# ln2's gain and bias for six of eight row tiles: from VectorE to GpSimd

## The chip, the cores and the metric

One NeuronCore of one Trainium2 chip. The metric is the device time of one execution in microseconds (us), the median over runs. Engines are named as the profile names them: PE is TensorE's matmul, PEld its weight load, DVE is VectorE, ACT is ScalarE, POOL is GpSimd, SP is the sync engine, which here only issues DMAs.

## The reference, cut to what matters

One post-norm layer over 1024 positions of width 1024, all in float32. The change lies in the very last step, the second residual update and its layer norm:

```python
y = (jax.nn.silu(a) * val) @ w_down[l]
x = _layer_norm(alpha * x + (1.0 + g2) * y, ln2_g[l], ln2_b[l])
```

`_layer_norm` takes mean and variance of each row over the 1024 columns, then `(x - mu) * rsqrt(var + eps) * gain + bias`. The gain `ln2_g` and the bias `ln2_b` are vectors over the columns; the kernel holds each of them copied to all 128 partitions, as `l2g` and `l2b` (128x1024 float32 each, in SBUF).

## The kernel before, in words

Everything up to the activation of the channel mixing (normalisation, projections, two attentions, merge, output projection, first residual norm, up-projection, convolution, gate) stands before the change and isn't touched. GpSimd's last work there is four DMA issues at 1334 to 1337 us; from then on its queue is empty to the end.

The down-projection that follows, from about 1337 us on, is one level of a fast matrix product: seven products P1, P5, P6, P3, P2, P7, P4 in place of eight, each over 11 pairs of operands (an activation block and a weight block or a sum of such, 128x512 each). A product's result is four tiles of 128 rows by 512 columns in PSUM (`psd`), in one of two sets of four banks; P1, P6, P7 and P4 add up in the same four banks.

Each operand is loaded from DRAM by SP (`rw`, nine buffers, line 1270) and split in two float32r parts in `op` (20 buffers, that is ten pairs): ScalarE writes the high part (line 1265, CAST), VectorE the low part (line 1266, `rw` minus the high part). Each pair then costs twelve matmuls: for each of the four row tiles high x high (line 1276), high x low (1277) and low x high (1278).

In the order in which the work is written, a product ends with line 1390, where VectorE adds the PSUM result to a kept tile. The rows of the output are 8 tiles `yt` of 128 rows by 1024 columns. P3 and P2 complete the two halves of row tiles 0 to 3, P7 the right half of tiles 4 to 7, P4 their left half. What follows from P3, P2 and P7 is put in a list (`later`), of which one entry is written after each pair of the next product: `part` (line 1314 gain `g2row`, line 1315 residual, line 1339 row statistics) and, for tiles 0 to 3, `finish`. P4's last nine pairs are handled tile by tile: all nine pairs for row tile 4, then for 5, 6, 7 (27 matmuls each), and behind each tile its left half (lines 1375, 1376, 1377) and its `finish`.

`finish` for tiles 0 to 5 is: some operations on 128x1 statistics (lines 121 to 139), ScalarE's normalisation of the whole 128x1024 tile in place (line 140), and then on VectorE a multiplication by `l2g` (line 1320) and an addition of `l2b` (line 1321), each 128x1024, in place. SP stores the tile (line 1331). For tiles 6 and 7 VectorE does the whole in two fused steps on halves (lines 1326 and 1327) and SP and ScalarE store a half each (line 1328).

A scheduler reads the written program and sets, ahead of the run, the order of the instructions on each engine; on the chip each engine then works through its own list in order. So what stands in front of an instruction in its engine's list delays it. Two dependences matter below. PE may start P4 on a PSUM bank only when line 1390 of P7 has read that bank, since P4 adds to the same bank. And line 1277 of a pair needs the low part that line 1266 wrote.

Of the kernel before, what the change touches and what calls it, by code (L numbers as in the profile page):

```python
# [15 lines left out]
ALU = mybir.AluOpType  # L16
# [28 lines left out]
def body(ctx, tc, a, out):  # L45
    nc = tc.nc
    ve, se, pe, po, sy = nc.vector, nc.scalar, nc.tensor, nc.gpsimd, nc.sync
# [67 lines left out]
    def norm_scale(src, n=2, st=None):  # L115
        if st is None:
            st = small.tile([P, n, 6], F32, name=nm("st"), tag=f"st{n}", bufs=4 if n == 2 else 1)
            for i in range(n):
                ve.bn_stats(out=st[:, i, :], in_=src[:, i * D // n : (i + 1) * D // n])
        mv = small.tile([P, 2], F32, name=nm("mv"), tag="mv")  # L120
        ve.bn_aggr(out=mv, in_=st.rearrange("p a b -> p (a b)"))
        v = small.tile([P, 1], F32, name=nm("v"), tag="v")
        ve.tensor_scalar_add(v, mv[:, 1:2], EPS)
        sd = small.tile([P, 1], F32, name=nm("sd"), tag="sd")
        se.activation(out=sd, in_=mv[:, 1:2], func=AF.Sqrt, bias=epst[:, 0:1])
        y = small.tile([P, 1], F32, name=nm("y"), tag="y")
        ve.reciprocal(out=y, in_=sd)
        t = small.tile([P, 1], F32, name=nm("t"), tag="t")
        ve.scalar_tensor_tensor(out=t, in0=y, scalar=v, in1=y, op0=ALU.mult, op1=ALU.mult)
        ve.tensor_scalar(out=t, in0=t, scalar1=-0.5, scalar2=1.5, op0=ALU.mult, op1=ALU.add)  # L130
        r = small.tile([P, 1], F32, name=nm("r"), tag="r")
        ve.tensor_tensor(out=r, in0=y, in1=t, op=ALU.mult)
        return mv, r

    def normalise(dst, src, on_act=False, st=None):
        mv, r = norm_scale(src, 2, st)
        if on_act:
            b = small.tile([P, 1], F32, name=nm("nb"), tag="nb")
            ve.scalar_tensor_tensor(out=b, in0=mv[:, 0:1], scalar=-1.0, in1=r, op0=ALU.mult, op1=ALU.mult)
            se.activation(out=dst, in_=src, func=AF.Identity, scale=r, bias=b)  # L140
        else:
            ve.tensor_scalar(out=dst, in0=src, scalar1=mv[:, 0:1], scalar2=r, op0=ALU.subtract, op1=ALU.mult)
# [53 lines left out]
    def halves(half):  # L196
        return slice(half * H, (half + 1) * H)
# [17 lines left out]
    class Stream:  # L215
# [49 lines left out]
        def finish(self, upto):  # L265
            while self.cur < upto:
                self.step()
# [1028 lines left out]
    with tc.tile_pool(name="dn", bufs=2, reuse_waits="tile") as dn:  # L1296
# [20 lines left out]
        def finish(t, y, st=None):  # L1317
            if t < NT - 2:
                normalise(y, y, True, st)
                ve.tensor_tensor(out=y, in0=y, in1=l2g, op=ALU.mult)  # L1320
                ve.tensor_tensor(out=y, in0=y, in1=l2b, op=ALU.add)
            else:
                mv, r = norm_scale(y, 2, st)
                for n in range(2):
                    ns = halves(n)
                    ve.scalar_tensor_tensor(out=y[:, ns], in0=y[:, ns], scalar=mv[:, 0:1], in1=l2g[:, ns], op0=ALU.subtract, op1=ALU.mult)
                    ve.scalar_tensor_tensor(out=y[:, ns], in0=y[:, ns], scalar=r, in1=l2b[:, ns], op0=ALU.mult, op1=ALU.add)
                    (sy, se)[n].dma_start(out=out[t * P : (t + 1) * P, ns], in_=y[:, ns])
# [12 lines left out]
        for p in products:  # L1341
# [17 lines left out]
            if p == "P5":  # L1359
                l2g = dn.tile([P, D], F32, name="l2g", tag="l2g", bufs=1)  # L1360
                l2b = dn.tile([P, D], F32, name="l2b", tag="l2b", bufs=1)
# [7 lines left out]
            for t in range(4):  # L1369
                for w in ws:  # L1370
                    down(ps, t, w, False, w is ws[-1], not fresh)
                if p == "P4":
                    z = dn.tile([P, H], F32, name=nm("z"), tag="z", bufs=2)
                    y, n0 = ys[4 + t], halves(0)
                    ve.tensor_tensor(out=z, in0=ps[t], in1=g2row[:, n0], op=ALU.mult)
                    ve.scalar_tensor_tensor(out=y[:, n0], in0=y[:, n0], scalar=ALPHA, in1=z, op0=ALU.mult, op1=ALU.add)
                    ve.bn_stats(out=stats[4 + t][:, 0, :], in_=y[:, n0])
                    finish(4 + t, y, stats[4 + t])
                    if t < 2:
                        sent(4 + t, y)  # L1380
            if p == "P1":
                p1 = kept("p1", ps)
            elif p == "P5":
                p5 = kept("p5", ps)
            elif p == "P6":
                u2 = kept("u2", ps)
            elif p in ("P3", "P2", "P7"):
                for t in range(4):
                    x = {"P3": u2, "P2": p1, "P7": p5}[p][t]
                    ve.tensor_tensor(out=x, in0=ps[t], in1=x, op=ALU.add)  # L1390
                    tt, n = {"P3": (t, 1), "P2": (t, 0), "P7": (4 + t, 1)}[p]
                    later.append(lambda tt=tt, n=n, x=x: part(tt, n, x))
                    if p == "P2":
                        later.append(lambda t=t: finish(t, ys[t], stats[t]))
# [65 lines left out]
```

## Time and profile before

| what | us |
|---|---|
| time, median of 3 runs | 1549.76 (1547.07 to 1550.41) |
| span of the profiled execution, first to last instruction | 1548.2 |
| median less the profiled span | 1.6 |
| PE busy, share of the span | 1502.7, 97% |
| DVE busy | 1034.5, 67% |
| ACT busy | 709.5, 46% |
| POOL busy | 658.2, 43% |
| lines 1320 and 1321 on DVE, six each | 7.2 and 7.1 |

The profiled execution is a single one, and its own time is given as the span alone; the time of a run contains what lies around the span too. Busy times are sums over the whole program, in which the stages have quite different limits: POOL's share all lies before 1337 us, and the change lies behind 1486 us. Rows of the timeline give the start, how long the instruction took, the engine, the line, what it writes and reads, and how many of them the row merges ("x4"). A merged row's length runs to the end of its last instruction; neighbours on DVE overlap by some 0.08 us, so the cost of an instruction in a busy stretch is read from start to start.

### The profile page before, as it was taken

The numbers are of one execution on the slowest core, as the hardware profiler recorded it, in microseconds if no ns is written. First come the engines' busy times: TensorE is split into PE (matmuls) and PEld (weight loads), VectorE is DVE, ScalarE is ACT, GpSimd is POOL, SyncE is SP. The second block draws the span as 40 slices with busy tenths as digits, with TensorE's granted clock in tenths as the row PEclk, the third lists the DMA queues.
The fourth block names the chain that finished last, engine by engine and source line by source line (L and its number), as shares of the span: only waits on it lengthen the run. The fifth ranks groups of instructions, "written<-read, shape, count | busy, mean of one in ns | idle before, by whom it ended". The sixth has DMA issues, their size and how long they took to land.

```text
span 1548.2 us, 21760 instructions
## 1 busy us (share of the span) xinstructions
PE 1502.7 (97%) x7663; PEld 1264.7 (82%) x7663; DVE 1034.5 (67%) x2038; ACT 709.5 (46%) x1316; POOL 658.2 (43%) x607
## 2 busy tenths in 40 slices
PE   6999999999999999999998999999999999999996
PEld 3788898889889888888886877888888888888885
DVE  6756566566656565554468587777778776845798
ACT  3545555554544454442112165544544554555451
POOL 0039897787878776730000005454455443000000
PEclk9999999999999999999999999999999999999998
DMA  9156666756576578758999575443344322697552
GB/s 366 50 165 215 217 192 198 218 194 216 189 233 220 189 260 299 260 151 292 308 323 347 214 258 190 140 154 132 122 140 147 115 102 104 246 328 255 191 190 75
DMA packets 129756, 317.54 MB, mean 205 GB/s; under 512 B 13024, under 2 KB 21936, under 8 KB 129648
## 3 DMA queue, kind: packets, MB, share of 16 engines
q1 hardware_dynamic: 90208, 197.83, 37.8%
q0 software_dynamic: 25344, 92.02, 17.8%
q10 hardware_dynamic: 14096, 26.31, 4.8%
q8 instruction: 60, 0.98, 0.3%
q14 instruction: 48, 0.39, 0.1%
HBM read 223.47 MB, written 84.25 MB: 199 GB/s over the span
## 4 chain that ended last, share of the span: by engine, by line
PE 72%; POOL 9%; DMA 8%; DVE 7%; issue 2%; ACT 1%; SPq 0%; ACTq 0%; DVEq 0%; POOLq 0%
PE psu L859 25%; PE psd L1277 4%; PE psd L1278 4%; PE psd L1276 4%; PE pso L508 3%; DMA wod<-dr 3%; PE psg L192 3%; PE psg L194 3%; PE psg L193 3%; POOL dr L553 2%; PE pst L494 2%; POOL acc L559 2%; POOL dr L556 2%; PE psq L194 2%; DMA brd<-dr 2%
## 5 line engine op out<-in xcount | busy, mean ns | idle before, releaser
L859 PE MATMUL psu<-hc,wx 128*128 128x512 f32 x792 | 185.7, 389 | 0.1
L859 PEld LDWEIGHTS psu<-hc,wx 128*128 128x128 f32 x792 | 148.6, 188 | 31.3 <-ACT u L1202 0.5
L1125 DVE SCALAR_TENSOR_TENSOR pcv<-u,convp,pcv 128x1024 f32<-128x1024 f32 x88 | 113.1, 1286 | 45.4 <-ACT pcv L1123 44.4
L1266 DVE TENSOR_TENSOR op<-rw,op 128x512 fp32r<-128x512 f32 x146 | 93.4, 687 | 52.8 <-ACT op L1265 52.5
L1265 ACT CAST op<-rw 128x512 fp32r<-128x512 f32 x146 | 85.2, 622 | 85.4 <-PE psd L1278 39.8
L457 ACT ACTIVATE s<-s,mx 128x640 f32<-128x640 f32 (+7 forms) x128 | 94.5, 738 | 58.6 <-DVE mx L451 57.4
L1277 PE MATMUL psd<-op,op 128*128 128x512 f32 x292 | 113.6, 389 | 0.9 <-DVE op L1266 0.9
L1278 PE MATMUL psd<-op,op 128*128 128x512 f32 x292 | 113.6, 389 | 0.0
L1276 PE MATMUL psd<-op,op 128*128 128x512 f32 x292 | 113.1, 389 | 0.0
L497 ACT CAST pt<-pst 128x512 fp32r<-128x512 f32 (+1 forms) x192 | 82.1, 450 | 62.3 <-PE pst L494 60.8
L498 DVE TENSOR_TENSOR pt<-pst,pt 128x512 fp32r<-128x512 f32 (+1 forms) x192 | 96.0, 519 | 17.2 <-ACT pt L497 15.5
L192 PE MATMUL psq<-h1h,wh 128*128 128x512 f32 x256 | 103.8, 407 | 1.7 <-DVE h1h L188 1.3
L192 PE MATMUL psg<-h1h,wh 128*128 128x512 f32 x256 | 103.7, 405 | 0.0
L194 PE MATMUL psq<-h1h,wl 128*128 128x512 f32 x256 | 100.9, 394 | 0.9 <-DVE wl L112 0.9
L194 PE MATMUL psg<-h1h,wl 128*128 128x512 f32 x256 | 100.3, 392 | 0.5 <-DVE wl L112 0.5
L193 PE MATMUL psq<-h1l,wh 128*128 128x512 f32 x256 | 100.8, 394 | 0.0
L193 PE MATMUL psg<-h1l,wh 128*128 128x512 f32 x256 | 100.2, 391 | 0.0
L556 POOL TENSOR_SCALAR dr<-dr,cond 128x512 f32<-128x512 f32 x56 | 89.9, 1607 | 8.1 <-DMA dr<-in_w_ada 7.1
L508 PE MATMUL pso<-pt,vs 128*128 128x256 f32 x608 | 90.4, 288 | 1.3 <-DVE pt L498 1.2
L994 POOL DMA_DIRECT2D xd<-xr x8 | 4.4, 545 | 199.3 <-DVE xr L992 199.3
L508 PEld LDWEIGHTS pso<-pt,vs 128*128 128x128 f32 x608 | 81.1, 191 | 8.7 <-DVE pt L498 2.6
L112 DVE TENSOR_TENSOR wl<-ws,wh 128x1024 fp32r<-128x1024 f32 x38 | 61.2, 1611 | 39.1 <-ACT wh L111 39.1
(286 smaller groups left out, 4001.3 us busy)
## 6 DMA issues: line engine op xcount, KB each, us to landing
ws<-in_w_up SPq DMA_DIRECT2D x34, 512.0 KB, 3.7
dr<-in_w_ada POOLq DMA_DIRECT2D x32, 512.0 KB, 4.8
dr<-in_w_down POOLq DMA_DIRECT2D x22, 512.0 KB, 4.8
td<-dr POOLq DMA_DIRECT2D x22, 512.0 KB, 4.7
rw<-td SPq DMA_DIRECT2D x44, 256.0 KB, 4.5
yd<-y SPq DMA_DIRECT2D x20, 512.0 KB, 2.7
rw<-yd SPq DMA_DIRECT2D x40, 256.0 KB, 4.2
rw<-sd SPq DMA_DIRECT2D x33, 256.0 KB, 4.6
```

Of the source, the lines that this page charges most:

```text
L192: pe.matmul(ps, wh, xh, start=start, stop=False)
L193: pe.matmul(ps, wh, xl, start=False, stop=False)
L194: pe.matmul(ps, wl, xh, start=False, stop=stop)
L457: se.activation(out=st[:, 0:nk], in_=st[:, 0:nk], func=AF.Exp, scale=-1.0, bias=prev, accum_out=sums[:, col : col + 1])
L498: ve.tensor_sub(out=dl, in0=src, in1=dh)
L508: pe.matmul(ps[:, 0:256], vs[:, h % 2, j0 + j, :], pt[j // 4][:, c, j % 4, :], start=j == 0 and c == 0, stop=j == nj - 1 and c == 1)
L556: po.tensor_scalar_mul(x[:, k % 2, :] if k else acc, x[:, k % 2, :], cond[:, k : k + 1])
L859: pe.matmul(ps, w[:, a_, k, :], h[k][b_], start=first, stop=k == 3 and a_ == 1, skip_group_check=on)
L1125: ve.scalar_tensor_tensor(out=ps, in0=u[b][:, 2 - d : S + 2 - d], scalar=cp[:, 2 - d : 3 - d], in1=ps, op0=ALU.mult, op1=ALU.add)
L1276: pe.matmul(ps[t], g[:, 0, ts], d[:, 0], start=start, stop=False, skip_group_check=on)
L1277: pe.matmul(ps[t], g[:, 0, ts], d[:, 1], start=False, stop=False, skip_group_check=on)
L1278: pe.matmul(ps[t], g[:, 1, ts], d[:, 0], start=False, stop=stop, skip_group_check=on)
```

## The change

Lines 1320 and 1321 are issued to GpSimd (`po`) where they were issued to VectorE (`ve`). Operands, shapes, tiles and results are the same: twelve instructions of 128x1024 float32, each with two inputs in SBUF.

```diff
         def finish(t, y, st=None):
             if t < NT - 2:
                 normalise(y, y, True, st)
-                ve.tensor_tensor(out=y, in0=y, in1=l2g, op=ALU.mult)
-                ve.tensor_tensor(out=y, in0=y, in1=l2b, op=ALU.add)
+                po.tensor_tensor(out=y, in0=y, in1=l2g, op=ALU.mult)
+                po.tensor_tensor(out=y, in0=y, in1=l2b, op=ALU.add)
             else:
```

The scheduler orders the end of the program anew. On POOL, behind the last DMA issue, the list now holds these rows; `yt_13419` to `yt_13425` are row tiles 0 to 3, `yt_13427` and `yt_13429` are tiles 4 and 5:

```order
+L1320 TENSOR_TENSOR yt_13419<-yt_13419,l2g 128x1024
+L1321 TENSOR_TENSOR yt_13419<-yt_13419,l2b 128x1024
+L1320 TENSOR_TENSOR yt_13421<-yt_13421,l2g 128x1024
+L1321 TENSOR_TENSOR yt_13421<-yt_13421,l2b 128x1024
+L1320 TENSOR_TENSOR yt_13423<-yt_13423,l2g 128x1024
+L1321 TENSOR_TENSOR yt_13423<-yt_13423,l2b 128x1024
+L1320 TENSOR_TENSOR yt_13425<-yt_13425,l2g 128x1024
+L1321 TENSOR_TENSOR yt_13425<-yt_13425,l2b 128x1024
+L1320 TENSOR_TENSOR yt_13427<-yt_13427,l2g 128x1024
+L1321 TENSOR_TENSOR yt_13427<-yt_13427,l2b 128x1024
+L1320 TENSOR_TENSOR yt_13429<-yt_13429,l2g 128x1024
+L1321 TENSOR_TENSOR yt_13429<-yt_13429,l2b 128x1024
```

Nothing else stands among or behind them on POOL. The second place is DVE where P7 ends and P4 begins; `psd_12900` and `psd_12901` are the PSUM tiles of row tiles 4 and 5, and `op_14625` to `op_14655` are the operands of P4's pairs 6, 7 and 8 out of 11 and the first of pair 9:

```order
 L1266 TENSOR_TENSOR op_14615<-rw_14616,op_14615 128x512
 L1266 TENSOR_TENSOR op_14620<-rw_14621,op_14620 128x512
+L1266 TENSOR_TENSOR op_14625<-rw_14626,op_14625 128x512
+L1266 TENSOR_TENSOR op_14630<-rw_14631,op_14630 128x512
+L1266 TENSOR_TENSOR op_14635<-rw_14636,op_14635 128x512
+L1266 TENSOR_TENSOR op_14640<-rw_14641,op_14640 128x512
+L1266 TENSOR_TENSOR op_14645<-rw_14646,op_14645 128x512
+L1266 TENSOR_TENSOR op_14650<-rw_14651,op_14650 128x512
+L1266 TENSOR_TENSOR op_14655<-rw_14656,op_14655 128x512
 L1390 TENSOR_TENSOR p_2484_13447<-psd_12900,p_2484_13447 128x512
 L1390 TENSOR_TENSOR p_2485_13449<-psd_12901,p_2485_13449 128x512
```

Seven low parts that stood behind line 1390 and the twelve instructions that follow from it (lines 1314, 1315, 1339) now stand in front of it. The four pairs of lines 1320 and 1321 of tiles 0 to 3, which stood among the low parts before this place, are gone from DVE, and so are those of tiles 4 and 5 near its end.

Two more lists change. PE's matmuls of P4 for row tile 4 were mixed with those of tile 5; they now stand ahead of them but for the last two (lines 1277 and 1278 of the last pair, `op_14675` and `op_14680`, which follow the second matmul of tile 5). On SP the stores of tiles 0 to 3 stood among the loads of P4's operands; they now stand behind the last of these loads.

## The prediction

> **What bounds the kernel now.** I read the page first, then the table of the last 70 us by stretches, then the timelines of VectorE and TensorE from 1486 us on.
>
> ```profile
> span 1548.2 us, 21760 instructions
> ...
> PE 1502.7 (97%) x7663; PEld 1264.7 (82%) x7663; DVE 1034.5 (67%) x2038; ACT 709.5 (46%) x1316; POOL 658.2 (43%) x607
> ```
>
> By the page TensorE bounds the program and VectorE has a third of its time free. That is an average. In the stretches (length, then busy time of PE, PEld, DVE, ACT and POOL) it is otherwise:
>
> ```profile
> 1486.00:1504.00 18.00, 18.00 (x81) 14.90 (x80) 18.00 (x33) 10.01 (x15) 0.00 (x0) 1.00 0.74 245
> 1504.00:1523.00 19.00, 19.00 (x86) 15.69 (x85) 17.96 (x31) 5.53 (x9) 0.00 (x0) 1.00 0.38 128
> ```
>
> From 1486 to 1523 us both TensorE and VectorE are full, and GpSimd does nothing. VectorE is behind with its work, not waiting for any; TensorE runs on operands that were made earlier. So a microsecond taken from VectorE here buys slack for TensorE, and a microsecond added is soon a stall of TensorE.
>
> The seam between P7 and P4 is where this is decided. VectorE around it (start, length, engine, line):
>
> ```profile
> 1486.69 2.36 DVE L1320 TENSOR_TENSOR yt<-yt,l2g 128x1024 f32<-128x1024 f32 x2
> 1488.96 2.36 DVE L1321 TENSOR_TENSOR yt<-yt,l2b 128x1024 f32<-128x1024 f32 x2
> 1491.23 0.15 DVE L130 TENSOR_SCALAR t<-t 128x1 f32<-128x1 f32 x1
> ...
> 1501.25 3.69 DVE L1266 TENSOR_TENSOR op<-rw,op 128x512 fp32r<-128x512 f32 x6
> 1504.86 2.48 DVE L1390 TENSOR_TENSOR p<-psd,p 128x512 f32<-128x512 f32 x4
> ```
>
> And TensorE, its first matmul of P4 and its last:
>
> ```profile
> 1506.19 0.39 PE L1276 MATMUL psd<-op,op 128*128 128x512 f32 x1
> ...
> 1535.89 0.39 PE L1278 MATMUL psd<-op,op 128*128 128x512 f32 x1
> ```
>
> P4 has 11 pairs x 12 = 132 matmuls, and 131 steps in 1535.89 - 1506.19 = 29.70 us make 0.227 us each, with no gap. The first of them needs the first line 1390. That ends at 1504.86 + 0.60 = 1505.5 us (four in 2.48 us), so the slack at the seam is 0.7 us.
>
> **The change, part by part.** *Removed from VectorE before the seam:* eight instructions. From 1486.69 to 1491.23 us four of them take 4.54 us, 1.14 each, so eight take 9.1 us. *Moved ahead of the seam:* seven low parts, at 3.61 / 6 = 0.60 us each (1501.25 to 1504.86), 4.2 us. If that were all, line 1390 would come 4.9 us sooner.
>
> *Added on GpSimd:* eight instructions before the seam. The profile has their like, line 793, an in-place product of two 128x1024 tiles in SBUF:
>
> ```profile
> L793 POOL TENSOR_TENSOR ost<-ost,ort x3: 2393/2397/3013, 659.5 to 680.9; 128x1024 f32<-128x1024 f32 x3
> ```
>
> I take 2.39 us (the third has a wait in it); eight make 19.1 us. GpSimd's queue holds nothing else, so their length alone would cost nothing: tiles 0 to 3 are stored long before the end. What costs is what VectorE can do meanwhile. Here are GpSimd and VectorE at 954 to 960 us, both with two-input work waiting:
>
> ```profile
> 953.80 1.27 POOL L848 TENSOR_TENSOR wh<-s,wh 128x512 fp32r<-128x512 f32 x1
> 955.04 1.28 POOL L848 TENSOR_TENSOR wl<-ws,wl 128x512 fp32r<-128x512 f32 x1
> 956.29 1.74 POOL L848 TENSOR_TENSOR wl<-s,wl 128x512 fp32r<-128x512 f32 x1
> ```
>
> ```profile
> 955.11 1.76 DVE L845 TENSOR_TENSOR wt<-ws,s 128x512 f32<-128x512 f32 x1 [1.77 <-POOL wh L848]
> 956.80 1.78 DVE L845 TENSOR_TENSOR wt<-ws,ws 128x512 f32<-128x512 f32 x1
> 958.50 0.68 DVE L1157 TENSOR_TENSOR u<-psu,p 128x512 f32<-128x512 f32 x1
> ```
>
> Line 845 takes 1.76 us where VectorE's like take 0.6: it starts at 955.11, GpSimd ends at 956.32, and 0.55 us later it is done. Then GpSimd's next takes 1.74 for 1.28: it waits for VectorE's. They take turns, one instruction at a time, and never overlap. Line 1157, with one input in PSUM, isn't held. Before the seam VectorE has almost only line 1266, with two inputs in SBUF. So while there is such work, every GpSimd instruction is lost to VectorE for its whole length.
>
> Line 1390 then comes at 1504.86 - 9.1 + 4.2 + 19.1 = 1519.1 us, 14.2 us later, and less the slack of 0.7 us TensorE stands for **13.5 us** at the seam. The bounds of this term are -4.9 us for VectorE, so none for TensorE, if nothing is held, and 14.2 us plus a few tenths if each change of turn costs some. I take the full hold, since the row with line 845 is the same pair of operations. Loads (SP) and the high parts (ACT) hide behind it: they keep ahead of VectorE, and the wait gives them more time. Moving the stores of tiles 0 to 3 behind the loads costs nothing, as nothing waits for these but the end.
>
> A second demand on VectorE agrees.
>
> ```profile
> 1514.45 7.30 DVE L1266 TENSOR_TENSOR op<-rw,op 128x512 fp32r<-128x512 f32 x12
> ```
>
> The last low part of P4 is done at 1521.75 us before (1514.45 + 7.30), so at 1521.75 + 19.1 - 9.1 = 1531.75 us after. Tile 4's matmuls now stand first, and want it about 80 matmuls from the end, at 1535.89 - 80 x 0.227 = 1517.7 us in the old time; with 13.5 us of delay and the next term it is wanted at 1533.7 us, and hidden.
>
> *TensorE's clock after the stall.* Where TensorE stood for longer before, it started again slowly:
>
> ```profile
> 840.43 0.80 PE L194 MATMUL psb<-oh,ws 128*128 128x512 f32 x1 [1.42 <-DMA ws<-brd]
> 841.02 0.63 PE L192 MATMUL psb<-oh,ws 128*128 128x512 f32 x1
> 841.45 0.63 PE L193 MATMUL psb<-ol,ws 128*128 128x512 f32 x1
> ...
> 846.08 0.40 PE L194 MATMUL psb<-oh,ws 128*128 128x512 f32 x1
> ```
>
> Behind a wait of 1.42 us the matmuls stand 0.43 us apart (841.02 to 841.45) until about 846.08. 5.65 us at that step in place of 0.227 lose 5.65 x (1 - 0.227 / 0.43) = 2.7 us. A stall of 13.5 us should end no better; I take **2.5 us**, with 0 and 3.2 us as bounds. The Trainium skill ("TensorE: Matmul & The Clock Gate", Part 1) has the clock halve after an idle window of about 3.4 us and come back after a busy one of the same length; by its 3.4 us the loss would be an estimated 1.6 us, and the row shows a longer one.
>
> *The end.* Behind the last matmul the work is VectorE's. A `z` starts 0.5 us behind the start of its last matmul:
>
> ```profile
> 1522.29 0.39 PE L1278 MATMUL psd<-op,op 128*128 128x512 f32 x1
> ```
>
> ```profile
> 1522.79 0.69 DVE L1375 TENSOR_TENSOR z<-psd,g2row 128x512 f32<-128x512 f32 x1 [1.04 <-PE psd L1278]
> ...
> 1533.68 0.68 DVE L1375 TENSOR_TENSOR z<-psd,g2row 128x512 f32<-128x512 f32 x1
> ...
> 1537.68 0.68 DVE L1375 TENSOR_TENSOR z<-psd,g2row 128x512 f32<-128x512 f32 x1
> ...
> 1543.51 1.42 DVE L1327 SCALAR_TENSOR_TENSOR yt<-yt,r,l2b 128x512 f32<-128x512 f32 x2
> ```
>
> Call E the start of the last matmul, 1535.89 before. The last tile's `z` starts at 1537.68, E + 1.8, since tile 6 was late: its own `z` (1533.68) stood behind the four instructions of tiles 4 and 5, some 4.6 us. VectorE ends at 1544.93, E + 9.0, and 1.4 us of that is tile 6's line 1327, which stood in the middle of tile 7's chain. If nothing is held, the last `z` starts at E + 0.5 and has no line 1327 of tile 6 in its chain: the end comes 1.3 + 1.3 = 2.6 us sooner after E. If lines 1326 and 1327 are held, GpSimd's second instruction of tile 5 decides. Tile 5's last matmul is at E - 54 x 0.227 = E - 12.2, its `z` at E - 11.7; its statistics and ScalarE's line 140 take some 6.3 us (from the first `z` at 1522.79 to the first line 1320, at 1533.68 - 4.6), GpSimd 4.8 and two turns of 0.6: E + 0.6. Only then comes tile 6's second line 1326 (0.7), three small ones (0.7) and two lines 1327 (1.4), so the last `z` starts at about E + 3.4 and the rest of its chain, without tile 6's line 1327, takes 9.0 - 1.8 - 1.4 = 5.8 us: E + 9.2. I take **+0.5 us**, with -2.6 and +1 as bounds.
>
> No row of this profile has a scalar_tensor_tensor beside a busy GpSimd, so which end holds isn't shown. The Trainium skill ("SBUF — State Buffer", Who interferes with whom) says that any VectorE instruction with two SBUF inputs contends with a GpSimd one that reads SBUF, and that the other fully blocks; by it lines 1326 and 1327 are held, while a rule for tensor_tensor alone would put the sum 3 us lower.
>
> *The sum.* 13.5 + 2.5 + 0.5 = 16.5 us, on the profiled span of 1548.2 us: 1564.7. The median of the runs is 1.6 us above that span, and I let it stay so: **1566.3 us**.
>
> **The rivals.**
>
> *VectorE's stream keeps the way (B).* One place shows another rule for the turns:
>
> ```profile
> 945.02 2.91 POOL L848 TENSOR_TENSOR wh<-ws,wh 128x512 fp32r<-128x512 f32 x1 [35.85 <-DMA p<-md]
> ```
>
> ```profile
> 944.88 1.29 DVE L1016 TENSOR_TENSOR hc<-ht,hc 128x512 fp32r<-128x512 f32 x2
> 946.09 0.69 DVE L848 TENSOR_TENSOR wl<-ws,wl 128x512 fp32r<-128x512 f32 x1
> 946.69 0.68 DVE L897 TENSOR_TENSOR mc<-psu,mc 128x512 f32<-128x512 f32 x1
> ```
>
> GpSimd waits through three two-input instructions at full speed, and gets its turn (1.27 us before 947.93) when line 897, with a PSUM input, comes. Against it: it is GpSimd's first after 36 us without work, and at 956 us the turns alternate. By this rule some of GpSimd's instructions slip to the lines 1390 and 1339, which read one SBUF tensor and cover about 2.4 us each (four at 0.6), so 4.8 of the 19.1 us are hidden. The bound is then the last low part: 1521.75 - 9.1 + 14.3 = 1527.0 against 1517.7 us, 9.3 us late, plus 0.5 at the end, and TensorE's waits come in pieces, with little of the slow clock: about 10 us, 1559.6 us.
>
> *Nothing is held (C), the other side.* GpSimd works beside VectorE, as it does beside line 1157. VectorE is 9.1 us lighter, TensorE runs on as before, and only the end moves: -2.6 us, 1547.2 us. It decides if a GpSimd instruction of 128x1024 leaves VectorE's two-input instructions alone. For it: GpSimd's queue is empty and VectorE's full. The Trainium skill ("Perfetto Trace Analysis", Optimizing Scalar/DVE Operations) says that with a saturated VectorE moving work to GpSimd may make sense, and warns in the same paragraph of the shared read port. Against it: the two lines 845.
>
> *GpSimd is slower still (D).* With the third row of line 793, 3.0 us each, eight take 24 us, and the seam costs 18.4 us: 1571 us. The row's length has a wait in it, which the turns already count, so I give it little.
>
> **How the numbers follow.** The forecast (A) 0.68, B 0.14, C 0.10, D 0.08. A's own range is 13.5 + 0 - 2.6 to 14.5 + 3.2 + 1, 1560.7 to 1568.5 us. With 1.7 us for the spread of the runs (1547.07 to 1550.41) and B taken in, the range is 1558.5 to 1570.5 us; it leaves out C and most of D. A difference of 0.2%, 3.1 us, is about what a measurement of this kernel can tell from none. C's 2.6 us lies inside that, and a little outside with the spread: faster 0.03, same 0.08, slower 0.89.
>
> **What would show it right or wrong.** Right: before the seam GpSimd's rows are 2.4 to 3.0 us and every line 1266 beside one takes 2 to 3 us, one per GpSimd row; the first line 1390 starts near 1519 us; TensorE has one gap of some 13 us in front of P4, then 0.43 us steps for 3 to 6 us; the last `z` starts 3 to 4 us behind the start of the last matmul. B: GpSimd rows far above 3 us, VectorE's at 0.7, and gaps of TensorE inside P4. C: no gap and line 1266 at 0.68 us. The forecast is wrong if line 1390 comes before 1512 us, or if TensorE's gap is there and the total isn't.

## The result and the profile after

The changed kernel takes 1562.7 us (median of 6 runs, 1559.48 to 1564.46), the kernel before 1548.41 us (6 runs, 1545.48 to 1550.41; three of them are those of the prediction, whose median was 1549.76). The ratio is 1.0088, with an interval of 1.0074 to 1.0103: 13.6 us slower by the ratio. The forecast was 1566.3 us, in a range from 1558.5 to 1570.5 us.

The page, first its span and then its busy times:

```profile
span 1561.9 us, 21769 instructions
...
PE 1505.8 (96%) x7663; PEld 1267.9 (81%) x7663; DVE 1045.2 (67%) x2026; ACT 708.2 (45%) x1316; POOL 688.8 (44%) x619
```

DVE issues 12 instructions fewer and is busy for 10.7 us more (1034.5 before). So the instructions left behind became longer. The stretches show where (length, then busy time of PE, PEld, DVE, ACT and POOL, then the clock granted to PE):

```profile
1486.00:1504.00 18.00, 18.00 (x81) 14.93 (x80) 18.00 (x17) 5.00 (x8) 16.33 (x6) 1.00 0.29 87
...
1505.42:1517.35 11.93, 0.16 (x2) 0.04 (x1) 11.93 (x14) 6.10 (x11) 4.53 (x2) 0.64 0.66 211
1517.35:1522.51 5.16, 5.16 (x12) 4.07 (x13) 5.16 (x9) 0.63 (x2) 0.00 (x0) 0.51 1.04 420
```

From 1486 to 1504 us DVE counts as busy for all 18 us in both kernels, but gets through 17 instructions in place of 33. A share of 100% hides that, a count does not. Then PE stands still (0.16 of the 11.93 us are the rest of P7's last matmul), and then runs for 5.16 us with a granted clock of 0.51.

PE in front of P4 and in its first matmuls (start, length), and its last matmul:

```profile
1505.19 0.39 PE L1278 MATMUL psd<-op,op 128*128 128x512 f32 x1
1517.35 0.76 PE L1276 MATMUL psd<-op,op 128*128 128x512 f32 x1 [11.77 <-DVE p L1390]
1517.91 0.63 PE L1277 MATMUL psd<-op,op 128*128 128x512 f32 x1
1518.34 0.63 PE L1278 MATMUL psd<-op,op 128*128 128x512 f32 x1
...
1522.51 0.39 PE L1276 MATMUL psd<-op,op 128*128 128x512 f32 x1
...
1549.51 0.39 PE L1278 MATMUL psd<-op,op 128*128 128x512 f32 x1
```

There is one gap, in front of P4, and line 1390 ends it. Then come steps of 0.43 us (1517.91 to 1518.34) up to 1522.51 us; from there on the steps are 0.227 us again, as in all of P4 before. GpSimd and VectorE ahead of the gap:

```profile
1485.75 2.51 POOL L1320 TENSOR_TENSOR yt<-yt,l2g 128x1024 f32<-128x1024 f32 x1 [149.19 <-ACT yt L140]
1488.34 2.72 POOL L1321 TENSOR_TENSOR yt<-yt,l2b 128x1024 f32<-128x1024 f32 x1
...
1504.61 2.67 POOL L1320 TENSOR_TENSOR yt<-yt,l2g 128x1024 f32<-128x1024 f32 x1 [2.05 <-ACT yt L140]
1507.36 2.67 POOL L1321 TENSOR_TENSOR yt<-yt,l2b 128x1024 f32<-128x1024 f32 x1
```

```profile
1486.03 2.78 DVE L1266 TENSOR_TENSOR op<-rw,op 128x512 fp32r<-128x512 f32 x1
1488.73 2.35 DVE L132 TENSOR_TENSOR r<-y,t 128x1 f32<-128x1 f32 x1
1491.00 0.68 DVE L1266 TENSOR_TENSOR op<-rw,op 128x512 fp32r<-128x512 f32 x1
...
1503.17 13.42 DVE L1266 TENSOR_TENSOR op<-rw,op 128x512 fp32r<-128x512 f32 x15
1516.52 2.47 DVE L1390 TENSOR_TENSOR p<-psd,p 128x512 f32<-128x512 f32 x4
```

Beside each GpSimd row one VectorE instruction is held until that row is over. Line 1266 takes 2.78 us where it takes 0.68 alone, and ends 0.55 us behind the first row (1488.81 against 1488.26 us), time for its own work. Line 132, a 128x1 operation of 0.15 us, takes 2.35 and ends with the second row (1491.08 against 1491.06). The merged row at 1503.17 us has two more in it, beside the last two GpSimd rows: 15 at 0.6 us would take 9.0 us, the row's length up to the next start is 13.35. Read from start to start, less 0.60 us for line 1266 and 0.07 to 0.12 for the small ones, the eight holds cost VectorE 2.10 (line 1266), 2.20 (132), 2.20 (139), 2.17 (129), 2.14 (1266) and 2.20 us (132), and twice 2.18 in that row: 17.4 us.

### The profile page after: what moved, and what is told of

It reads as the page before. It is cut to its first block, busy times and chain, and to the rows that moved or that the text cites. A ratio compares the mean times of both kernels' runs of the same rounds, so it can differ in the third digit from the quotient of the medians.

```text
span 1561.9 us, 21769 instructions
## 1 busy us (share of the span) xinstructions
PE 1505.8 (96%) x7663; PEld 1267.9 (81%) x7663; DVE 1045.2 (67%) x2026; ACT 708.2 (45%) x1316; POOL 688.8 (44%) x619
## 4 chain that ended last, share of the span: by engine, by line
PE 86%; DVE 8%; DMA 3%; ACT 1%; issue 1%; SPq 0%; DVEq 0%; ACTq 0%
PE psu L859 26%; PE pso L508 5%; PE psg L192 4%; PE psg L194 4%; PE psg L193 4%; PE pst L494 4%; PE psd L1277 3%; PE psd L1276 3%; PE psd L1278 3%; PE psq L192 3%; PE psq L194 3%; PE psq L193 3%; PE pss L443 2%; PE pss L442 2%; PE psv L295 2%; PE psv L294 2%
## 5 line engine op out<-in xcount | busy, mean ns | idle before, releaser
L1266 DVE TENSOR_TENSOR op<-rw,op 128x512 fp32r<-128x512 f32 x146 | 101.8, 746 | 52.9 <-ACT op L1265 52.5
L556 POOL TENSOR_SCALAR dr<-dr,cond 128x512 f32<-128x512 f32 x56 | 93.2, 1666 | 8.8 <-DMA dr<-in_w_ada 7.8
L1320 POOL TENSOR_TENSOR yt<-yt,l2g 128x1024 f32<-128x1024 f32 x6 | 15.8, 2633 | 180.4 <-ACT yt L140 180.4
```

Source lines behind the costliest of these rows:

```text
L1266: ve.tensor_sub(out=w[:, 1], in0=st, in1=w[:, 0])
```

## The experiments

Theory: GpSimd and VectorE take turns, whole instructions, as long as both have two inputs in SBUF; each of the eight GpSimd instructions ahead of P4 is lost to VectorE, and the stall, the slow clock and the end follow. The rivals: the new order does it (the low parts ahead of line 1390, tile 4's matmuls first); or any work of GpSimd on these tiles; or it isn't the clock that makes P4's start slow. All edits are made in the changed kernel, and each time stands beside runs of the kernel before on the same chip (medians 1548.66 us for the first four kernels, 1549.42 us for the last three). A difference in microseconds is the ratio's, times that median.

**Only tiles 4 and 5 on GpSimd.**

```diff
-                po.tensor_tensor(out=y, in0=y, in1=l2g, op=ALU.mult)
-                po.tensor_tensor(out=y, in0=y, in1=l2b, op=ALU.add)
+                eng = po if t >= 4 else ve
+                eng.tensor_tensor(out=y, in0=y, in1=l2g, op=ALU.mult)
+                eng.tensor_tensor(out=y, in0=y, in1=l2b, op=ALU.add)
```

> Lines 1320 and 1321 on GpSimd for row tiles 4 and 5 alone, on VectorE for tiles 0 to 3. Theory (the hold: while a two-input GpSimd instruction runs, VectorE's instructions with two SBUF inputs stand still, 2.2 us for each of 128x1024): the eight GpSimd instructions in front of the seam are gone, so TensorE has no gap before P4, and only the end differs: VectorE is 4.6 us lighter there and is held four times, wholly or in part, so -1 to +4 us against the kernel before. Rival 1 (the order, not the hold: the seven low parts moved ahead of line 1390 make the stall): the order at the seam is the old one, so no gap either, same figure. Rival 2 (GpSimd's slowness in the last chain is what costs): most of the 14 us is still there.

Measured: 1551.67 us, ratio 1.0028 (1.0009 to 1.0047), +4.3 us (1.4 to 7.3; the medians are 3.0 us apart). P4 starts without a gap. The end is worse than in the changed kernel. GpSimd, then VectorE, then the last matmul (line numbers are one higher here):

```profile
1533.87 2.40 POOL L1321 TENSOR_TENSOR yt<-yt,l2g 128x1024 f32<-128x1024 f32 x1 [192.11 <-ACT yt L140]
...
1541.94 2.67 POOL L1322 TENSOR_TENSOR yt<-yt,l2b 128x1024 f32<-128x1024 f32 x1
```

```profile
1539.62 2.79 DVE L1327 SCALAR_TENSOR_TENSOR yt<-yt,mv,l2g 128x512 f32<-128x512 f32 x1
1542.33 2.29 DVE L129 SCALAR_TENSOR_TENSOR t<-y,v 128x1 f32<-128x1 f32 x1
...
1546.37 0.68 DVE L1376 TENSOR_TENSOR z<-psd,g2row 128x512 f32<-128x512 f32 x1
...
1550.87 1.41 DVE L1328 SCALAR_TENSOR_TENSOR yt<-yt,r,l2b 128x512 f32<-128x512 f32 x2
```

```profile
1540.60 0.39 PE L1278 MATMUL psd<-op,op 128*128 128x512 f32 x1
```

Here tiles 4 and 5 are finished together, and GpSimd's four rows reach to 1544.61 us, 4.0 us behind the start of the last matmul. Tile 6's instructions are held meanwhile, and the last `z` starts 5.8 us behind that matmul and VectorE ends 11.7 us behind it, 2.7 us later than before. The rest of the 4.3 us lies within the interval. The measured 4.3 us lie just above what was expected (-1 to +4), and the interval reaches well into it; the end is late for the reason that the prediction gave. Line 1327, a scalar_tensor_tensor with two SBUF inputs, takes 2.79 us where it takes 0.73 alone, so it is held as well, which the prediction had no row for.

**Only tiles 0 to 3 on GpSimd.** The same edit with `t < 4`.

> Lines 1320 and 1321 on GpSimd for row tiles 0 to 3 alone, on VectorE for tiles 4 and 5. Theory (the hold): the gap of TensorE before P4 is there with 12 us, the slow matmuls behind it cost 2.4 us, the end is as before to within 1 us: +13 to +15 us against the kernel before. Rival 2 (the last chain is what costs): 0 to +2 us.

Measured: 1564.25 us, ratio 1.0101 (1.0081 to 1.0122), +15.6 us. PE at the seam:

```profile
1507.11 0.39 PE L1278 MATMUL psd<-op,op 128*128 128x512 f32 x1
1519.28 0.76 PE L1276 MATMUL psd<-op,op 128*128 128x512 f32 x1 [11.78 <-DVE p L1391]
...
1523.15 0.39 PE L1276 MATMUL psd<-op,op 128*128 128x512 f32 x1
```

The step is 12.17 us, that of the changed kernel 12.16. The eight instructions ahead of P4 make the whole stall. With those of tiles 4 and 5 added the time is no longer: in the changed kernel tile 4's matmuls stand first, and GpSimd is done with tile 5 about when the last matmul starts. The slow matmuls end after 3.9 us here (the last row), in the changed kernel after 5.2.

**None on either engine.** Lines 1320 and 1321 left out for tiles 0 to 5.

```diff
                 normalise(y, y, True, st)
-                po.tensor_tensor(out=y, in0=y, in1=l2g, op=ALU.mult)
-                po.tensor_tensor(out=y, in0=y, in1=l2b, op=ALU.add)
```

> The multiplications and additions of ln2's rows are left out for row tiles 0 to 5, on both engines; tiles 6 and 7 as they were. The order on VectorE at the seam is that of the changed kernel, with the seven low parts ahead of line 1390. Theory (the hold): no gap before P4, VectorE 9.1 us lighter there, and at the end the last z starts 0.5 us behind the last matmul: -2 to -3 us against the kernel before. Rival 1 (the order makes the stall): a gap of several us before P4 stays, +5 us or more.

Measured: 1546.94 us, ratio 0.9987 (0.9968 to 1.0005), -2.0 us. VectorE at the seam, and the last tile's `z`:

```profile
1504.46 0.69 DVE L1266 TENSOR_TENSOR op<-rw,op 128x512 fp32r<-128x512 f32 x1 [1.43 <-ACT op L1265]
1505.07 2.48 DVE L1388 TENSOR_TENSOR p<-psd,p 128x512 f32<-128x512 f32 x4
...
1536.50 0.69 DVE L1373 TENSOR_TENSOR z<-psd,g2row 128x512 f32<-128x512 f32 x1 [0.20 <-PE psd L1278]
```

As in the changed kernel, all but five of P4's low parts stand ahead of line 1390 (here 1388). With the work gone and no hold, VectorE is ahead of ScalarE and waits 1.43 us for it, the moved low parts included, and TensorE has no gap in front of P4. So the order isn't the cause. It also gives the ceiling: even moved free of charge the twelve instructions would bring about 2 us (at most 5.0 by the interval's lower end; 4.2 in the kernel with fills below, which leaves them out too), hardly more than a measurement of this kernel can tell. No kernel here that does the whole work beats the kernel before.

**A third GpSimd instruction for each of tiles 0 to 3.** Four more of the same kind ahead of P4.

```diff
                 po.tensor_tensor(out=y, in0=y, in1=l2b, op=ALU.add)
+                if t < 4:
+                    po.tensor_tensor(out=y, in0=y, in1=l2g, op=ALU.mult)
```

> The changed kernel with one more multiplication by l2g on GpSimd for each of row tiles 0 to 3 (twelve GpSimd instructions before the seam in place of eight). Theory (the hold, 2.2 us for each): 8.8 us more at the seam, a gap of 20 to 21 us, +22 to +24 us against the kernel before. Rival 1 (the order): the same as the changed kernel, +14 us.

Measured: 1571.2 us, ratio 1.0146 (1.0122 to 1.0171), +22.6 us. PE at the seam:

```profile
1508.48 0.39 PE L1278 MATMUL psd<-op,op 128*128 128x512 f32 x1
1529.29 0.76 PE L1276 MATMUL psd<-op,op 128*128 128x512 f32 x1 [20.42 <-DVE p L1392]
...
1534.91 0.40 PE L1277 MATMUL psd<-op,op 128*128 128x512 f32 x1
```

The step is 20.81 us, 8.65 more than the changed kernel's 12.16, so 2.16 us for each instruction added: the same dose as that of the eight before them.

**GpSimd instructions with one input.** The product with `l2g` and the sum with `l2b` are replaced by two scalings by a per-row number.

```diff
-                po.tensor_tensor(out=y, in0=y, in1=l2g, op=ALU.mult)
-                po.tensor_tensor(out=y, in0=y, in1=l2b, op=ALU.add)
+                po.tensor_scalar_mul(y, y, cond[:, 0:1])
+                po.tensor_scalar_mul(y, y, cond[:, 0:1])
```

> On GpSimd, in place of lines 1320 and 1321, two multiplications of the tile by a 128x1 column each (one input tensor in place of two; the gain and bias of row tiles 0 to 5 are left out). Reading 1 (any GpSimd instruction that reads SBUF holds VectorE's two-input ones for its whole length): with 128x512 of this form at 1.6 us in the kernel before, eight of 3.1 us hold 24 us, a gap of 18 us or more before P4, +18 to +22 us against the kernel before. Reading 2 (only a second GpSimd input collides): as with nothing on GpSimd, no gap, -2 to -3 us. Between them, if it holds for a part of its length, a gap of a few us.

Measured: 1547.2 us, ratio 0.9989 (0.9973 to 1.0004), -1.7 us, as without the instructions, though a GpSimd row lasts 2.85 us or more, as long as with two inputs. GpSimd and VectorE:

```profile
1488.98 2.85 POOL L1321 TENSOR_SCALAR yt<-yt,cond 128x1024 f32<-128x1024 f32 x1
1491.80 8.36 POOL L1320 TENSOR_SCALAR yt<-yt,cond 128x1024 f32<-128x1024 f32 x1
```

```profile
1489.02 1.09 DVE L129 SCALAR_TENSOR_TENSOR t<-y,v 128x1 f32<-128x1 f32 x1
...
1492.04 5.50 DVE L1266 TENSOR_TENSOR op<-rw,op 128x512 fp32r<-128x512 f32 x9
1498.32 2.00 DVE L1266 TENSOR_TENSOR op<-rw,op 128x512 fp32r<-128x512 f32 x3 [0.79 <-ACT op L1265]
```

The time is that of reading 2, but the rows are neither of the two clean outcomes. Beside the row at 1488.98 us the 128x1 operation is held for 0.9 us (1.09 for 0.21), not for the 2.85 us of the row. And at 1491.80 us GpSimd waits: nine line 1266 run past it at full speed until 1497.54, and it ends 2.6 us later. The holds cost no time, since VectorE is still early enough to wait for ScalarE, 0.79 us in the next row. How GpSimd reads in this form was not settled.

**GpSimd only writes.** Two fills of the tile in place of the two instructions.

```diff
-                po.tensor_tensor(out=y, in0=y, in1=l2g, op=ALU.mult)
-                po.tensor_tensor(out=y, in0=y, in1=l2b, op=ALU.add)
+                po.memset(y, 0.0)
+                po.memset(y, 1.0)
```

> On GpSimd, in place of lines 1320 and 1321, two memsets of the tile (no input; the outputs of row tiles 0 to 5 are constants). Theory (VectorE's second input collides with what GpSimd reads): nothing is held, no gap before P4, -2 to -3 us against the kernel before, as with nothing on GpSimd. Rival (the whole of GpSimd's access collides, writes too): each memset holds VectorE for its length, a gap if eight of them last over 5 us in all.

Measured: 1545.46 us, ratio 0.9973 (0.9958 to 0.9988), -4.2 us; the interval overlaps that of the kernel without the instructions, so I read no more out of it. GpSimd, and VectorE beside it:

```profile
1484.15 0.96 POOL L1321 MEMSET yt<- 128x1024 f32 x1
```

```profile
1484.12 0.69 DVE L1266 TENSOR_TENSOR op<-rw,op 128x512 fp32r<-128x512 f32 x1
```

Nothing is held. What costs is not work on GpSimd as such, but what it reads.

**Matmuls to fill the gap.** 48 matmuls that nobody reads, in the other four banks, ahead of P4.

```diff
+            if p == "P4":
+                g, d = ws[-1]
+                for j in range(48):
+                    pe.matmul(bank_b[j % 4], g[:, 0, 0:P], d[:, 0], start=True, stop=True, skip_group_check=True)
```

> The changed kernel with 48 more matmuls, whose results nothing reads, between P7 and P4, so that TensorE works through 10.9 of the 12.2 us of its gap. Theory (a stall of this length also lowers the granted clock, 2.4 us behind it): the first line 1390 comes when it did, P4's matmuls follow at 0.227 us from the first on, 2.4 us less than the changed kernel, +11 to +12.5 us against the kernel before. Rival (the slow matmuls come from the operands or from the seam itself): no change against the changed kernel, +14 us.

Measured: 1561.75 us, ratio 1.0089 (1.0057 to 1.0121); against the changed kernel's ratio of 1.0088 the interval is too wide for a difference of 2 us. The trace shows the mechanism. Two stretches across the seam, PE's first matmuls of P4 and two later ones, and GpSimd's first row:

```profile
1507.00:1519.00 12.00, 12.00 (x55) 9.93 (x54) 12.00 (x14) 7.08 (x11) 5.45 (x2) 1.00 0.57 177
1518.00:1525.00 7.00, 6.00 (x27) 4.69 (x26) 7.00 (x13) 3.19 (x6) 0.00 (x0) 1.00 0.96 332
```

```profile
1521.21 0.47 PE L1276 MATMUL psd<-op,op 128*128 128x512 f32 x1 [1.00 <-DVE p L1394]
1521.51 0.40 PE L1277 MATMUL psd<-op,op 128*128 128x512 f32 x1
...
1532.47 0.40 PE L1276 MATMUL psd<-op,op 128*128 128x512 f32 x1
1533.11 0.50 PE L1277 MATMUL psd<-op,op 128*128 128x512 f32 x1 [0.24 <-DVE op L1266]
```

```profile
1489.50 2.51 POOL L1320 TENSOR_TENSOR yt<-yt,l2g 128x1024 f32<-128x1024 f32 x1 [149.19 <-ACT yt L140]
```

VectorE is as late as in the changed kernel: P4 starts 31.7 us behind GpSimd's first row here (1489.50 to 1521.21), 31.6 us there (1485.75 to 1517.35). But PE was busy up to 1.0 us before, the granted clock stays 1.00 and the first step is 0.30 us where it was 0.56. From P4's first matmul to its last it takes 30.6 us, in the changed kernel 32.2 and before 29.7. So 1.6 us are won and not the 2.4 expected; 0.8 of the 0.9 us left over lie between 1531.50 and 1533.44 us, around a wait for a low part inside P4 and at a granted clock of 1.00. So the slow start is the clock, and it follows from the stall.

## Why the prediction was right, and where it was off

**The turns, the core of the forecast.** Right in kind: the rows in pairs, the dose of the third instruction, and nothing held beside fills. Rival C (nothing held, 1547.2 us) describes the kernel that leaves the instructions out (1546.94 us), not the changed one. Rival B asked for GpSimd rows far above 3 us and gaps inside P4; with two inputs the rows are 2.5 to 2.9 us and there is one gap. B's rule does show with one input, in the row of 8.36 us. Why GpSimd waited through three two-input instructions at 945.02 us, the row that B rests on, stays open. Rival D's 3.0 us each is excluded by 2.16 us in the dose.

**The stall at the seam, 13.5 us: mis-sized, 11.9 us.** The step that was off is "every GpSimd instruction is lost to VectorE for its whole length", taken as 2.39 us. The eight holds took 17.4 us, not 19.1, so 2.2 us each. The four more in the experiment cost 2.16 us each, so the size isn't a chance of this execution. By the prediction's own sum, 1504.86 - 9.1 + 4.2 + 17.4, line 1390 comes at 1517.4 us; this execution came to the seam 0.8 us earlier (P7's last matmul at 1505.19, before at 1506.19 - 0.23 = 1505.96), which leaves 1516.6, and 1516.52 is measured. The rows show where the 0.2 us go: GpSimd's second row ends 2.25 us behind the line 1266 that it waited for (1488.81 to 1491.06), so some 0.14 of its 2.39 us pass beside VectorE's work, and some 0.05 us of the held instruction's pass beside GpSimd's (the first line 1266 is done 0.55 us behind the row, and costs 0.60 in a busy stretch). What GpSimd does in the 0.14 us was not tried. The slack was mis-read too, the other way: P4's first matmul starts 0.23 us behind the end of the first line 1390 (1516.52 + 0.60 = 1517.12 to 1517.35), so of the 0.7 us only 0.5 were slack.

**The slow clock, 2.5 us: right, with luck in the size.** 12 steps in 1522.51 - 1517.35 = 5.16 us where 12 x 0.227 = 2.72 us would do: 2.4 us. Other executions came out otherwise: with tiles 0 to 3 alone, behind a step of 12.17 us, it was 9 slow steps in 3.87 us (1519.28 to 1523.15), 1.8 us lost; with the third instruction 13 in 5.62 us (1529.29 to 1534.91), 2.7 us lost. The estimate of 1.6 us by the Trainium skill's window ("TensorE: Matmul & The Clock Gate", Part 1) was too small in all three: the clock came back after 3.9 to 5.6 us, not 3.4; the row at 840 us had 5.65.

**The end, +0.5 us: right in its mechanism, +0.1 us.** GpSimd's rows for tiles 4 and 5, and VectorE beside them:

```profile
1537.20 2.40 POOL L1320 TENSOR_TENSOR yt<-yt,l2g 128x1024 f32<-128x1024 f32 x1 [27.17 <-ACT yt L140]
...
1544.36 2.39 POOL L1320 TENSOR_TENSOR yt<-yt,l2g 128x1024 f32<-128x1024 f32 x1 [1.95 <-ACT yt L140]
1546.82 2.73 POOL L1321 TENSOR_TENSOR yt<-yt,l2b 128x1024 f32<-128x1024 f32 x1
```

```profile
1537.70 0.69 DVE L1375 TENSOR_TENSOR z<-psd,g2row 128x512 f32<-128x512 f32 x1 [1.85 <-PE psd L1278]
...
1543.81 0.69 DVE L1375 TENSOR_TENSOR z<-psd,g2row 128x512 f32<-128x512 f32 x1 [0.82 <-PE psd L1278]
1544.54 2.76 DVE L1376 SCALAR_TENSOR_TENSOR yt<-yt,z 128x512 f32<-128x512 f32 x1
1547.33 0.70 DVE L1377 BATCH_NORM_STATS2 st<-yt 128x6 f32<-128x512 f32 x1
...
1548.38 1.72 DVE L1326 SCALAR_TENSOR_TENSOR yt<-yt,mv,l2g 128x512 f32<-128x512 f32 x1
...
1552.70 0.69 DVE L1375 TENSOR_TENSOR z<-psd,g2row 128x512 f32<-128x512 f32 x1
...
1557.20 1.42 DVE L1327 SCALAR_TENSOR_TENSOR yt<-yt,r,l2b 128x512 f32<-128x512 f32 x2
```

E is 1549.51 us. GpSimd ends tile 5 at E + 0.0 (forecast E + 0.6), the last `z` starts at E + 3.2 (E + 3.4), VectorE ends at E + 9.1 (E + 9.2; before E + 9.0). Lines 1376 and 1326 are held, as the Trainium skill's rule for two SBUF inputs has it ("SBUF — State Buffer", Who interferes with whom). The prediction takes from it that the held one is fully blocked; the rows with two inputs agree, those with one input on GpSimd's side do not (0.9 us of 2.85). Without a hold the end would be near E + 6.4, where it is in the kernel that leaves the instructions out (`z` at 1536.50, 0.4 us behind its last matmul). Two things in the prediction's account of the end are wrong. Its working gives E + 9.2 against E + 9.0, that is +0.2 us; the +0.5 of its sum is not worked out. And the profile before does have rows of a scalar_tensor_tensor beside a busy GpSimd: two of line 1125 from 976.61 us on, the second beside GpSimd's line 848 at 977.68, take 2.62 us, and 2.61 with GpSimd idle (1330.29). But one of their inputs is in PSUM, so they leave open what happens with two in SBUF.

**The sum.** 11.9 + 2.5 for P4's length (32.16 in place of 29.70) + 0.1 - 0.8 for the earlier seam = 13.7 us, and the spans differ by 1561.9 - 1548.2 = 13.7. The forecast was 3.6 us too high: 1.6 at the seam (the shorter holds, less what the slack gave back), 0.4 from the end, 0.8 from the profiled execution being early at the seam, and 0.8 because the median lies 0.8 us above the span here and not 1.6.

## What to carry to other kernels

Before moving a VectorE instruction with two SBUF inputs to GpSimd, look at what VectorE has queued beside it: if that has two SBUF inputs too, the move adds time there, here 2.2 us held for 1.14 us saved, even when VectorE's average over the program leaves a third free. Look for it in the count of instructions in a stretch and in the length of the smallest ones, not in the busy share, which counts the hold as work. And price the stall with what it does to TensorE's clock: here 12 us of stall cost 2.4 us more, and 1.8 in the kernel with tiles 0 to 3 alone.

## What the runs showed of the hardware

- The hold doesn't depend on the size of what is held: 128x1 operations with two inputs took 2.35 us for 0.15, 2.2 us lost as with a 128x512 one. Four of the eight holds ahead of P4 fell on such operations.
- tensor_tensor and scalar_tensor_tensor are held alike (line 1376: 2.76 us for 0.69). Operations with one SBUF tile to read beside PSUM, or one alone, are not: `z` took 0.69 us beside GpSimd's row at 1537.20 us and 0.69 with GpSimd done (1552.70), and the statistics took 0.70 us beside the row at 1546.82.
- A GpSimd instruction with one tile input (2.85 us for 128x1024) held a VectorE operation for 0.9 us, and was itself passed by nine VectorE instructions in a row (8.36 us); a GpSimd fill (0.96 us) held none.
